# Projections q, k, v in banks of 512 columns, merged small operations, and squares summed by TensorE, in a two-layer encoder on one core

## The chip, the core and the metric

The kernel runs on one core of a Trainium2 chip. It has five engines with instruction streams of their own: TensorE (PE in the profile; its weight loads are listed as PEld), VectorE (DVE), ScalarE (ACT), GpSimd (POOL) and SyncE (SP, which issues the transfers). They meet through semaphores. On-chip tiles have 128 partitions; TensorE adds into 8 banks of PSUM, each of 128 x 512 fp32. The metric is device microseconds (us) of one execution, lower is better.

## What is computed

An encoder of two layers over 512 tokens of width 1024. A layer, cut to what matters here:

```
h = rms_norm(x, norm1_g[l]) * (1.0 + sc1) + sh1
proj = h @ w_in[l]
da_q, da_k, da_v, dn_q, dn_k, dn_v, dn_z, dn_b, dn_a, gates = split(proj)
q = apply_rope(rms_norm(q, qn_gain)); k = apply_rope(rms_norm(k, kn_gain))   # 4 heads x 2 maps x 64
p = softmax(q k^T * d**-0.5); a = p[map 0] - lam * p[map 1]; y_a = rms_norm(a @ v) ...
y_b = gated_deltanet(dn_q, dn_k, dn_v, dn_z, dn_b, dn_a)   # conv of 5 taps, chunks of 64, 4 heads, 2 directions
x = x + gt1 * ((g_a * (y_a @ w_branch_a) + g_b * (y_b @ w_branch_b)) @ w_out)
h = rms_norm(x, norm2_g[l]) * (1.0 + sc2) + sh2
x = x + gt2 * (square(relu(h @ w_mlp1)) @ w_mlp2)
```

## The kernel before

Every fp32 operand of a large product is split in a high part, rounded to the format that TensorE multiplies fast, and the low rest (hh and hl for the activations, whi and wlo for the weights, uho and ulo in the second matrix of the MLP). A product is three matmuls: hh with whi, hl with whi, hh with wlo. ScalarE makes a high part, VectorE the rest. Weights arrive in chunks of 512 KB (raw_*), 128 x 1024 elements each.

The program doesn't run in the order in which it is written. Every operation is recorded in a plan, and a list scheduler (`Plan.schedule`) puts the operations of each engine in one fixed order, from estimated costs and from levels of urgency; `Plan.issue` writes them out, so every instruction in the profile stands on line 431 and is told by its tiles. An engine works its list off strictly in that order. Pools of tiles (F for weights, Y for activations, Z for small vectors, B for the 8 banks) and limits on groups (three banks for dense products, group "d"; four chunks each of raw, whi and wlo) are part of the plan. The string ORDER (line 490), one per layer, sets the order in which the pieces of the middle of a layer are recorded: q, k, v are the projections for attention (`da_qk`, `da_v`); d is the projection of one delta-rule head and its convolution (`dn_proj`: the bank is d_dn, the running sum on VectorE is cacc, its SiLU times it is kqv); a, b, c are the steps of the delta rule (`gdn_a`, `gdn_b`, `gdn_c`); z its gate, t attention of one head. The digit is the head, or in q, k, v before the half of the columns.

- `da_dense(kind, j)` (line 801) makes one of q, k, v for 256 of its 512 columns: two chunks of 4 k-blocks x 256 columns, two banks (tokens 0 to 255 and 256 to 511, two 256-column token tiles in each), 96 matmuls. There are 12 such calls, 1152 matmuls.
- `da_qk` takes each bank: ScalarE squares it (dsq), VectorE sums the squares (dass), multiplies by cosine (rot) and by sine (dt, twice), GpSimd adds. Then `rsqrt` makes the scale (dars) from dass: a chain of 12 small VectorE operations (tiles rqv, rqu, rqr) by bit tricks and Newton steps. For k GpSimd multiplies rot by it, for q it goes into qsc. TensorE transposes rot (qkT).
- `gdn_a` needs a head's kqv: products of k with itself (kk) and q (kq), transposes (tokT, qT), another `rsqrt`, small scales (gsv, gsL and others, one operation for each of the two directions d), and L.
- `attention` has, for each of 16 tiles of queries a layer, a reciprocal of two sums (rc), a copy (r), and two multiplications (cc) before the two softmax maps are joined (pr).
- `norm` needs the sum of squares of the new x over the 1024 features. `square` (line 616) lets ScalarE square each of the 8 blocks per token half (nsq) and VectorE add it to a running sum; one matmul against ones per 128 tokens (nss) finishes it, `rsqrt` follows, nrb spreads the result over partitions, and xn, hh, hl are made. At the boundary of the layers the last blocks come out of `finish` (line 1443) one by one: transposes yT, xT, square.

Of the kernel before, what the change touches and what calls it, by code (L numbers as in the profile page):

```python
# [17 lines left out]
P = 128  # L18
# [149 lines left out]

class Eng:
# [15 lines left out]
class Plan:  # L185
# [68 lines left out]
    def schedule(self):  # L254
# [9 lines left out]
        dve_rows, dve_end = None, -OTHER_ROWS  # L264
        order = []
# [53 lines left out]
        while todo:  # L319
# [117 lines left out]
OTHER_ROWS = 110.0  # L437
DMA_LEAD, DMA_TAIL, DMA_STEP, DMA_DEPTH = 1100.0, 2400.0, 475.0, 8
# [12 lines left out]
def cost(eng, fn, dst, ins, kw):  # L451
# [21 lines left out]
    if fn == "memset":  # L473
# [4 lines left out]
NF, NY, NZ = 20, 58, 64  # L478
# [11 lines left out]
ORDER = ("q0 d0 a0 d1 a1 d2 a2 d3 a3 b0 k0 z0 c0 z1 c1 k1 z2 q1 v0 t0 z3 t1 c3 c2 v1 t2 t3",  # L490
         "d0 q0 k0 d1 a1 d2 a0 a2 d3 a3 b0 z0 c0 z1 c1 k1 z2 c2 v0 t0 q1 z3 v1 c3 t2 t3 t1")
# [3 lines left out]
def encoder(ctx, tc, a, out):  # L495
# [120 lines left out]
    def square(first, xk, hf):  # L616
# [156 lines left out]
    for l in range(DEPTH):  # L773
# [27 lines left out]
        def da_dense(kind, j):  # L801

            ch = [chunk(a["w_da"][l, 2 * kind + j, i], f"da{kind}{j}{i}") for i in range(2)]
            pss = [B([P, 2, 256], "d_da", grp="d") for tp in range(2)]
            for i in range(2):
                wh, wl = ch[i]
                for t in range(NT):
                    for k in range(4 * i, 4 * i + 4):
                        for n, (xx, w) in enumerate(((hh, wh), (hl, wh), (hh, wl))):
                            acc(pss[t // 2], t % 2, xx[k][:, t * P:(t + 1) * P], w[k % 4],  # L810
                                t % 2 == 1 and k == NK - 1 and n == 2, level=DENSE)
            return pss

        def da_qk(kind, j):
            for tp, ps in enumerate(da_dense(kind, j)):
                pl.level = EVAC
                tt = slice(2 * tp, 2 * tp + 2)
                X = ps.rearrange("p t (g d) -> p t g d", d=64)
                sq = Y([P, 8, 64], "dsq", keep=KEEP1)
                act.activation(sq.rearrange("p g d -> p (g d)"), ps.rearrange("p t c -> p (t c)"), AF.Square)  # L820
                ss = Z([P, 8], "dass")
                dve.reduce_sum(ss, sq, axis=AX.X)
                t1 = Y([P, 2, 4, 64], "rot", keep=KEEP1)
                t2 = Y([P, 2, 4, 64], "dt2", keep=KEEP1)
# [13 lines left out]
                pt = B([P, 2, 2, P], "qkT")
                for h2 in range(2):
                    for t in range(2):  # L840
                        pe.transpose(pt[:, h2, t], t1[:, t, 2 * h2:2 * h2 + 2].rearrange("p m d -> p (m d)"), ident)
                xt = Y([P, 2, 256], "qkst", keep=KEEP1)
                act.copy(xt, pt.rearrange("p h t f -> p h (t f)"))
                sp.dma_start(out=qkd[kind][:, 2 * j:2 * j + 2, 256 * tp:256 * tp + 256], in_=xt)
                pl.level = CHAIN

        def da_v(j):
            for tp, ps in enumerate(da_dense(2, j)):
                vs_ = Y([P, 2, 256], "vst", keep=KEEP1)
                act.copy(vs_, ps, level=EVAC)  # L850
                gate["v"] = sp.dma_start(out=vtd[:, 2 * tp:2 * tp + 2, 256 * j:256 * j + 256], in_=vs_, level=EVAC)
# [120 lines left out]
        def gdn_a(h, XA):  # L972
# [17 lines left out]
            for d in range(2):  # L990
                dve.tensor_tensor(out=sv[:, d], in0=rk, in1=beta[:, d, :, h], op=ALU.mult)
# [562 lines left out]
```

## Time and profile before

| | us |
|---|---|
| median of 3 runs | 1637.55 |
| lowest, highest run | 1634.5, 1638.19 |
| the profiled execution's own time | 1637.45 |
| span of its trace, first to last instruction | 1635.7 |
| TensorE busy in the span | 1597.4 (98%) |
| VectorE busy | 1314.3 (80%) |
| ScalarE busy | 829.7 (51%) |
| GpSimd busy | 164.9 (10%) |

The profile gives, for one execution, the busy time of each engine, the chain of work that ended last followed back from the end, the waits of an engine with what released it, and single instructions on a timeline with their start and duration in us. The windows view gives busy times between two moments and the granted clock of TensorE as a share of full speed (PEclk). A matmul's own duration overlaps its neighbours', so the rate of a stream is read from an unbroken stretch of it on the chain: its time over its count.

### The profile page before, as it was taken

To read this page: it belongs to the slowest core of one execution; us is meant where nothing else is said; L and a number is where in the kernel's file an instruction comes from. 1 tells how busy PE (TensorE), PEld (TensorE's weight loads), DVE (VectorE), ACT (ScalarE), POOL (GpSimd) and SP (SyncE) were. 2 spreads that over 40 slices of the span, in tenths; PEclk is the share of its full clock that TensorE was granted. 3 is DMA by queue.
4 is the path that set the end of the run, shared out by engine and by line. 5 is a ranking of instruction groups with operands and counts; after the bars stand their busy time and mean duration, and the time that the engine had idled before them with its cause. 6 is when DMAs were issued, how large, how long until landed. Compare 5 with 4: busy or idle time off the path is not lost.

```text
span 1635.7 us, 25251 instructions
## 1 busy us (share of the span) xinstructions
PE 1597.4 (98%) x9136; PEld 1385.3 (85%) x9136; DVE 1314.3 (80%) x2878; ACT 829.7 (51%) x1591; POOL 164.9 (10%) x170
## 2 busy tenths in 40 slices
PE   6989999999999999999989899999999999999998
PEld 5869988888899888888879799998888988888887
DVE  7999969899899988585998897699527885767676
ACT  4583335573266545454558442467423674636361
POOL 0253201000300000000005221000003000000000
PEclk9989999999999999999989999999999999999999
DMA  9423465538767483436233323422343525252542
GB/s 376 165 75 120 136 221 145 170 116 296 284 251 290 173 303 121 162 122 235 96 129 123 111 90 109 131 69 81 103 142 129 206 91 189 94 191 92 192 168 77
DMA packets 107726, 260.77 MB, mean 159 GB/s; under 512 B 27841, under 2 KB 40769, under 8 KB 107602
## 3 DMA queue, kind: packets, MB, share of 16 engines
q1 hardware_dynamic: 107602, 259.16, 46.1%
q8 instruction: 72, 1.18, 0.3%
q14 instruction: 52, 0.43, 0.1%
HBM read 242.31 MB, written 16.81 MB: 158 GB/s over the span
## 4 chain that ended last, share of the span: by engine, by line
PE 93%; DVE 4%; ACT 1%; issue 0%; DMA 0%; POOL 0%; SPq 0%; DVEq 0%; ACTq 0%
PE d_m L431 19%; PE d_g L431 11%; PE m2x L431 11%; PE d_da L431 8%; PE d_dn L431 6%; PE d_out L431 6%; PE m2y L431 5%; PE d_m1f L431 3%; PE d_z L431 3%; PE m2z L431 3%; PE d_brb L431 3%; PE d_bra L431 3%; PE sc L431 2%; PE px L431 2%; PE po L431 2%; PE pv L431 2%
## 5 line engine op out<-in xcount | busy, mean ns | idle before, releaser
L431 PE MATMUL d_m<-hh,whi_m 128*128 128x512 f32 x448 | 174.5, 389 | 0.0
L431 PE MATMUL d_m<-hl,whi_m 128*128 128x512 f32 x448 | 174.4, 389 | 0.0
L431 PE MATMUL d_m<-hh,wlo_m 128*128 128x512 f32 x448 | 174.4, 389 | 0.0
L431 DVE TENSOR_TENSOR m2lo<-m,m2hi 128x1024 fp32r<-128x1024 f32 x112 | 132.9, 1221 | 13.1 <-ACT m2hi L431 8.6
L431 ACT CAST m2hi<-m 128x1024 fp32r<-128x1024 f32 x112 | 114.8, 1048 | 50.1 <-DMA m<-in_w_m_dram 20.2
L431 DVE SCALAR_TENSOR_TENSOR ada<-ada,cb 128x1024 f32<-128x1024 f32 x96 | 116.5, 1227 | 2.6 <-DMA ada<-in_ada_w_dram 2.6
L431 PE MATMUL d_da<-whi_da,hh 128*128 128x256 f32 x384 | 109.4, 285 | 0.0
L431 PE MATMUL d_da<-whi_da,hl 128*128 128x256 f32 x384 | 109.1, 284 | 0.0
L431 PE MATMUL d_da<-wlo_da,hh 128*128 128x256 f32 x384 | 108.8, 285 | 0.0
L431 ACT ACTIVATE relu<-d_m 128x512 f32<-128x512 f32 x56 | 33.5, 598 | 147.8 <-PE d_m L431 147.8
L431 PE MATMUL d_g<-hh,wlo_g 128*128 128x512 f32 x256 | 102.0, 399 | 0.0
L431 PE MATMUL d_g<-hl,whi_g 128*128 128x512 f32 x256 | 102.0, 399 | 0.0
L431 PE MATMUL d_g<-hh,whi_g 128*128 128x512 f32 x256 | 102.0, 398 | 0.0
L431 PEld LDWEIGHTS d_m<-hh,wlo_m 128*128 128x128 f32 x448 | 84.1, 188 | 17.4
L431 PEld LDWEIGHTS d_m<-hh,whi_m 128*128 128x128 f32 x448 | 84.1, 188 | 17.4
L431 PEld LDWEIGHTS d_m<-hl,whi_m 128*128 128x128 f32 x448 | 84.1, 188 | 17.4
L431 PE MATMUL d_dn<-hh,whi_dn 128*128 128x512 f32 (+1 forms) x208 | 78.4, 387 | 2.6 <-DVE L L431 2.6
L431 PE MATMUL d_dn<-hh,wlo_dn 128*128 128x512 f32 (+1 forms) x208 | 79.3, 385 | 1.6 <-DVE wlo_dn L431 1.6
L431 DVE TENSOR_TENSOR u<-relu 128x256 f32<-128x256 f32 x64 | 27.1, 423 | 66.8 <-ACT relu L431 66.5
L431 PE MATMUL d_dn<-hl,whi_dn 128*128 128x512 f32 (+1 forms) x208 | 80.5, 387 | 0.0
L431 ACT CAST whi_m<-raw_m 128x1024 fp32r<-128x1024 f32 x56 | 58.7, 1049 | 42.3 <-DMA raw_m<-in_w_mlp_dram 35.7
L431 DVE TENSOR_TENSOR wlo_m<-raw_m,whi_m 128x1024 fp32r<-128x1024 f32 x56 | 67.9, 1221 | 12.6 <-ACT whi_m L431 12.4
(326 smaller groups left out, 4777.9 us busy)
## 6 DMA issues: line engine op xcount, KB each, us to landing
m<-in_w_m_dram SPq DMA_DIRECT2D x112, 512.0 KB, 4.3
ada<-in_ada_w_dram SPq DMA_DIRECT2D x96, 512.0 KB, 6.1
raw_m<-in_w_mlp_dram SPq DMA_DIRECT2D x56, 512.0 KB, 4.6
raw_g<-in_w_g_dram SPq DMA_DIRECT2D x32, 512.0 KB, 4.4
raw_out<-in_w_out_dram SPq DMA_DIRECT2D x32, 512.0 KB, 4.3
raw_dn<-in_w_dn_dram SPq DMA_DIRECT2D x24, 512.0 KB, 6.3
raw_da<-in_w_da_dram SPq DMA_DIRECT2D x24, 512.0 KB, 3.9
xs<-xT SPq DMA_DIRECT2D x24, 256.0 KB, 2.5
```

Of the source, the lines that this page charges most:

```text
L431: op.ins = getattr(eng[op.eng[0]], fn)(*[real(v) for v in op.args], **{k: real(v) for k, v in op.kw.items()})
```

## The change

1. `da_dense(kind)` makes all 512 columns of q, k or v at once: four chunks of 2 k-blocks x 512 columns, which stay through two passes, one for each pair of token tiles; a pass fills two banks of one token tile x 512 columns. A matmul has 512 columns, 96 for one kind in one layer, 576 in all. Six calls stand where twelve stood.
2. `da_qk` joins `rsqrt` for the two banks of a pass: 8 chains on 128x16 in place of 16 on 128x8 (12 operations each), 4 qsc in place of 8.
3. `gdn_a` makes gsv and gsL for both directions in one operation each: 16 in place of 32.
4. `attention` takes the reciprocal of the second sum alone and joins the two cc multiplications; the first sum's reciprocal is taken once for a head: 64 operations fewer, 8 added. In all VectorE has 2604 instructions in place of 2784, TensorE 7786 in place of 8354.
5. At the end of layer one the second token half's last four squares are not added by VectorE; TensorE sums them: 20 nss instructions in place of 12 at the boundary and 4 nsq additions fewer.
6. The planner's ORDER, two pool sizes (F 20 to 21, Y 58 to 56) and the estimate for narrow fp32 products are new; so all that stands in the middle of a layer has another order.

```diff
-ORDER = ("q0 d0 a0 d1 a1 d2 a2 d3 a3 b0 k0 z0 c0 z1 c1 k1 z2 q1 v0 t0 z3 t1 c3 c2 v1 t2 t3",
-         "d0 q0 k0 d1 a1 d2 a0 a2 d3 a3 b0 z0 c0 z1 c1 k1 z2 c2 v0 t0 q1 z3 v1 c3 t2 t3 t1")
+ORDER = ("q0 d0 d2 a2 a0 d1 a1 d3 a3 b0 k0 z1 z0 c0 z2 c2 c1 v0 z3 c3 t0 t3 t2 t1",
+         "q0 d0 d1 a0 d2 a1 a2 d3 k0 a3 b0 z0 c0 z1 z2 c1 v0 t3 c2 z3 c3 t2 t0 t1")
@@ square @@
-    def square(first, xk, hf):
+    def square(first, xk, hf, apart=False):
 
         sq = Y([P, S // 2], "nsq")
         act.activation(sq, xk[:, HALF[hf]], AF.Square)
         if first:
             nsum[hf] = [sq]
+        elif apart:
+            nsum[hf].append(sq)
         else:
             dve.tensor_tensor(out=nsum[hf][0], in0=nsum[hf][0], in1=sq, op=ALU.add)
...
@@ da_dense, da_qk @@
-        def da_dense(kind, j):
-
-            ch = [chunk(a["w_da"][l, 2 * kind + j, i], f"da{kind}{j}{i}") for i in range(2)]
-            pss = [B([P, 2, 256], "d_da", grp="d") for tp in range(2)]
-            for i in range(2):
-                wh, wl = ch[i]
-                for t in range(NT):
-                    for k in range(4 * i, 4 * i + 4):
...
+        def da_dense(kind):
+
+            ch = [chunk(a["w_da"][l, kind, i], f"da{kind}{i}") for i in range(4)]
+            for tp in range(2):
+                pss = [B([P, 512], "d_da", grp="d") for b in range(2)]
+                for i, (wh, wl) in enumerate(ch):
+                    for b, ps in enumerate(pss):
+                        ts = slice((2 * tp + b) * P, (2 * tp + b + 1) * P)
+                        for k in range(2 * i, 2 * i + 2):
+                            for n, (xx, w) in enumerate(((hh, wh), (hl, wh), (hh, wl))):
+                                pe.matmul(ps, lhsT=xx[k][:, ts], rhs=w[k % 2], start=k == 0 and n == 0,
+                                          stop=k == NK - 1 and n == 2, level=DENSE)
+                yield tp, pss
...
-                ss = Z([P, 8], "dass")
-                dve.reduce_sum(ss, sq, axis=AX.X)
...
+                ss, rs = Z([P, 2, 8], "dass"), Z([P, 2, 8], "dars")
...
                 rsqrt(rs, ss, 1.0 / 64)
...
@@ gdn_a @@
-            for d in range(2):
-                dve.tensor_tensor(out=sv[:, d], in0=rk, in1=beta[:, d, :, h], op=ALU.mult)
-                dve.scalar_tensor_tensor(out=sL[:, d], in0=sv[:, d], scalar=-1.0, in1=rk, op0=ALU.mult, op1=ALU.mult)
+            dve.tensor_tensor(out=sv, in0=beta[:, :, :, h], in1=bc(rk, 1, 2), op=ALU.mult)
+            dve.scalar_tensor_tensor(out=sL, in0=sv, scalar=-1.0, in1=bc(rk, 1, 2), op0=ALU.mult, op1=ALU.mult)
@@ attention @@
-                rc, cc = Z([P, 2], "rc"), Z([P, 1], "cc")
-                dve.reciprocal(rc, sums)
-                dve.tensor_copy(r0[:, qt:qt + 1], rc[:, 0:1])
-                dve.tensor_tensor(out=cc, in0=sums[:, 0:1], in1=rc[:, 1:2], op=ALU.mult)
-                dve.tensor_tensor(out=cc, in0=cc, in1=nlam, op=ALU.mult)
+                rc, cc = Z([P, 1], "rc"), Z([P, 1], "cc")
+                dve.reciprocal(rc, sums[:, qt, 1:2])
+                dve.scalar_tensor_tensor(out=cc, in0=sums[:, qt, 0:1], scalar=nlam, in1=rc, op0=ALU.mult, op1=ALU.mult)
...
+            dve.reciprocal(r0, sums[:, :, 0])
@@ finish @@
-                            square(m == 4 * th, xT[m], th)
+                            square(m == 4 * th, xT[m], th, th and i == 0)
```

Three places show how the planned order moves. A row is a line of the program, the operation, its output and inputs by tile and number, its size, and "xN" where N equal rows follow each other.

**VectorE in layer one, convolutions of the delta-rule heads.** In the kernel before, these rows follow the scales of the second head; kqv1_1144 and kqv0_1162 are that head's.

```order
L431 SCALAR_TENSOR_TENSOR ada0_16_450,mod0_160<-ada0_16_450,cb_103 128x1024
L431 SCALAR_TENSOR_TENSOR kqv1_1144<-kqv1_1144,cacc_770 128x512
L431 SCALAR_TENSOR_TENSOR kqv0_1162<-kqv0_1162,cacc_867 128x512
L431 COPY tok1_1179<-tokT_1169 128x512
L431 SCALAR_TENSOR_TENSOR cacc_1166<-d_dn2_876,cols_88,cacc_1166 128x510
L431 SCALAR_TENSOR_TENSOR cacc_1173<-d_dn1_975,cols_88,cacc_1173 128x510
```

The same place in the changed kernel:

```order
L444 TENSOR_SCALAR qsc_880<-dars_1106 128x2x4x2
L444 SCALAR_TENSOR_TENSOR ada0_16_450,mod0_160<-ada0_16_450,cb_103 128x1024
L444 SCALAR_TENSOR_TENSOR kqv2_1144<-kqv2_1144,cacc_910 128x512
L444 SCALAR_TENSOR_TENSOR cacc_1149<-d_dn1_1060,cols_88,cacc_1149 128x510
L444 SCALAR_TENSOR_TENSOR cacc_1155<-d_dn1_328,cols_88,cacc_1155 128x510
L444 COPY tok2_1172<-tokT_1162 128x512
L444 SCALAR_TENSOR_TENSOR cacc_1149<-d_dn1_1060,cols_88,cacc_1149 128x511
L444 SCALAR_TENSOR_TENSOR cacc_1155<-d_dn1_328,cols_88,cacc_1155 128x511
L444 SCALAR_TENSOR_TENSOR cacc_1149<-d_dn1_1060,cols_88,cacc_1149 128x511
```

The scales of the whole of q stand ahead now, and the sum over the late bank d_dn1_1060 stands in front of the sum over d_dn1_328, a bank that TensorE fills much earlier.

**TensorE in layer two, around the second head's kk.** Before, with two projections (d_dn2_9769, d_dn1_9794) begun and the third weight parts not yet used, and the transposes qkT of k's first half behind it:

```order
L431 MATMUL d_dn2_9769<-hl0_8828,whi_dn20_9737 128x512
L431 MATMUL d_dn1_9794<-hh0_8821,whi_dn10_9747 128x512
L431 MATMUL d_dn1_9794<-hl0_8828,whi_dn10_9747 128x512
L431 MATMUL kk_9808<-kqv1_9799 128x128 x4
L431 MATMUL tokT_9819<-cst_86,kqv1_9799 128x128 x4
L431 MATMUL d_dn0_9835<-hh0_8821,whi_dn00_9757 128x512
L431 MATMUL d_dn0_9835<-hl0_8828,whi_dn00_9757 128x512
L431 MATMUL d_dn2_9769<-hh0_8821,wlo_dn20_9829 128x512
L431 MATMUL d_dn2_9769<-hh1_8841,whi_dn20_9737 128x512
L431 MATMUL d_dn2_9769<-hl1_8857,whi_dn20_9737 128x512
L431 MATMUL qkT_9854<-cst_86,rot_9587 128x128 x2
```

In the changed kernel:

```order
L444 MATMUL d_dn2_9199<-hl6_8507,whi_dn20_9135 128x512
L444 MATMUL d_dn2_9199<-hh6_8500,wlo_dn20_9181 128x512
L444 MATMUL d_dn2_9199<-hh7_8505,whi_dn20_9135 128x512
L444 MATMUL d_dn2_9199<-hl7_8512,whi_dn20_9135 128x512
L444 MATMUL kk_9279<-kqv1_9264 128x128 x4
L444 MATMUL tokT_9291<-cst_86,kqv1_9264 128x128 x4
L444 MATMUL d_dn2_9199<-hh7_8505,wlo_dn20_9181 128x512
L444 MATMUL d_dn1_9299<-hh0_8429,whi_dn10_9144 128x512
L444 MATMUL d_dn1_9299<-hl0_8444,whi_dn10_9144 128x512
L444 MATMUL d_dn1_9299<-hh0_8429,wlo_dn10_9284 128x512
```

The kk stands at the end of a full projection, with no qkT behind it: all of q has been made ahead of it, and k comes later.

**TensorE at the boundary of the layers.** Before:

```order
L431 MATMUL yT<-cst,y_6490 128x128 x4
L431 MATMUL m2y<-m2lo,uho 128x512
L431 MATMUL yT<-cst,y_6517 128x128
L431 MATMUL nrb<-cst,nrs 128x128 x2
L431 MATMUL yT<-cst,y_6517 128x128 x3
L431 MATMUL nss<-ones,nsq 128x1 x2
L431 MATMUL d_ba<-hh_8821,w_ba 32x256
L431 MATMUL d_dn_8836<-hh_8821,whi_dn_8638 128x256
L431 MATMUL d_ba<-hl_8828,w_ba 32x256
L431 MATMUL d_dn_8836<-hl_8828,whi_dn_8638 128x256
```

In the changed kernel:

```order
L444 MATMUL yT<-cst,y_6071 128x128 x4
L444 MATMUL yT<-cst,y_6098 128x128 x4
L444 MATMUL nss<-ones,nsq 128x1 x2
L444 MATMUL nrb<-cst,nrs 128x128 x2
L444 MATMUL nss<-ones,nsq 128x1 x8
L444 MATMUL d_ba<-hh_8429,w_ba 32x256
L444 MATMUL d_da<-whi_da_8230,hh_8429 128x512 x2
L444 MATMUL d_ba<-hl_8444,w_ba 32x256
```

Eight nss stand between the last transposes and the next layer's first products, and 512-column products of q on the first token half stand where 256-column products of the delta rule's projection stood.

## Rows read from the trace of the kernel before

**Rows 1.** The page: span, busy time and share of engines, the chain by engine.

```profile
span 1635.7 us, 25251 instructions
PE 1597.4 (98%) x9136; PEld 1385.3 (85%) x9136; DVE 1314.3 (80%) x2878; ACT 829.7 (51%) x1591; POOL 164.9 (10%) x170
PE 93%; DVE 4%; ACT 1%; issue 0%; DMA 0%; POOL 0%; SPq 0%; DVEq 0%; ACTq 0%
```

**Rows 2.** Windows: stretch, busy us of PE, PEld, DVE, ACT, POOL; clock; DMA; GB/s.

```profile
50.00:135.60 85.60, 79.36 (x433) 67.04 (x432) 78.85 (x226) 57.50 (x159) 27.12 (x27) 0.92 0.29 91
135.60:372.00 236.40, 236.40 (x1682) 212.67 (x1681) 208.34 (x621) 116.57 (x274) 34.53 (x40) 1.00 0.48 150
...
820.00:850.00 30.00, 24.70 (x160) 22.19 (x160) 26.17 (x79) 18.59 (x43) 3.58 (x6) 0.83 0.42 147
850.00:912.00 62.00, 55.09 (x374) 50.72 (x373) 51.03 (x159) 42.00 (x114) 28.16 (x23) 0.96 0.27 88
912.00:1160.00 248.00, 248.00 (x1711) 223.00 (x1710) 213.51 (x639) 126.22 (x308) 31.85 (x44) 1.00 0.34 104
```

**Rows 3.** Pieces of the chain, in order: start us, us, what.

```profile
179.03 18.60 PE d_da L431 x155
...
577.70 43.52 PE d_m L431 x192
...
980.78 13.44 PE d_da L431 x112
```

**Rows 4.** Waits of TensorE, 95 to 135 us: us in total, times, longest us.

```profile
PE d_dn L431 <- DVE L L431: 2.6, 1, 2.6
PE qT L431 <- DVE kqv L431: 1.9, 1, 1.9
PE tokT L431 <- DVE kqv L431: 1.7, 1, 1.7
```

**Rows 5.** Costliest groups, VectorE and ScalarE: count | busy us, mean ns of one | idle before.

```profile
L431 DVE TENSOR_TENSOR wlo_da<-raw_da,whi_da 128x1024 fp32r<-128x1024 f32 x24 | 29.2, 1218 | 1.6 <-ACT whi_da L431 1.6
L431 DVE TENSOR_TENSOR dt<-d_da,sgn 128x256 f32<-128x256 f32 x32 | 12.7, 414 | 0.0
L431 DVE TENSOR_REDUCE dass<-dsq 128x8 f32<-128x512 f32 x16 | 11.4, 716 | 1.4 <-ACT dsq L431 1.4
L431 DVE TENSOR_TENSOR rot<-d_da,cg 128x512 f32<-128x512 f32 x16 | 10.9, 684 | 1.4 <-ACT dsq L431 1.4
L431 DVE TENSOR_TENSOR cc<-sums,rc 128x1 f32<-128x1 f32 x32 | 5.6, 175 | 0.0
L431 ACT ACTIVATE dsq<-d_da 128x512 f32<-128x512 f32 x16 | 9.5, 599 | 21.6 <-PE d_da L431 20.2 <-issue 1.4
```

**Rows 6.** Waits of TensorE, 850 to 912 us.

```profile
PE kk L431 <- DVE rqr L431: 3.6, 1, 3.6
PE qkT L431 <- POOL rot L431: 1.7, 1, 1.7
PE d_dn L431 <- DVE wlo_dn L431: 1.6, 1, 1.6
```

**Rows 7.** Timeline there: start us, duration us, instruction, [wait before it].

```profile
897.73 0.24 DVE L431 SCALAR_TENSOR_TENSOR rqu<-rqr 128x8 f32<-128x8 f32 x2
904.39 4.77 POOL L431 TENSOR_TENSOR rot<-rot,dars 128x512 f32<-128x512 f32 x2 [9.02 <-DVE dars L431]
```

**Rows 8.** Waits of TensorE, 820 to 850 us.

```profile
PE nss L431 <- DVE nsq L431: 3.4, 1, 3.4
PE yT L431 <- DVE y L431: 1.9, 1, 1.9
```

**Rows 9.** Timeline there.

```profile
831.87 0.42 ACT L431 ACTIVATE nsq<-xT 128x256 f32<-128x256 f32 x1 [0.31 <-DVE xT L431]
833.08 0.42 DVE L431 TENSOR_TENSOR nsq<-nsq 128x256 f32<-128x256 f32 x1
833.64 0.99 PE L431 MATMUL nss<-ones,nsq 128*128 128x1 f32 x4 [3.42 <-DVE nsq L431]
```

More of the change, by code (lines that the diff above doesn't have):

```diff
@@ L370, in schedule @@
                     s = max(s, dve_end + OTHER_ROWS)
+            elif e == "pe":
+                rows = op.form()
+                if rows != pe_form:
+                    s = max(s, pe_end + OTHER_FORM)
             if e == "pe":
@@ L396, in schedule @@
                     dve_rows, dve_end = rows, op.end
+                elif e == "pe":
+                    pe_form, pe_end = rows, op.end
             order.append(op)
@@ L437 @@
 OTHER_ROWS = 110.0
+OTHER_FORM = 0.0
 DMA_LEAD, DMA_TAIL, DMA_STEP, DMA_DEPTH = 1100.0, 2400.0, 475.0, 8
@@ new lines, in da_qk @@
+        def da_qk(kind):
+            for tp, pss in da_dense(kind):
+                pl.level = EVAC
+                ss, rs = Z([P, 2, 8], "dass"), Z([P, 2, 8], "dars")
+                t1s = []
+                for b, ps in enumerate(pss):
+                    t = 2 * tp + b
+                    X = ps.rearrange("p (g d) -> p g d", d=64)
+                    sq = Y([P, 8, 64], "dsq", keep=KEEP1)
+                    act.activation(sq.rearrange("p g d -> p (g d)"), ps, AF.Square)
+                    dve.reduce_sum(ss[:, b], sq, axis=AX.X)
+                    t1 = Y([P, 8, 64], "rot", keep=KEEP1)
+                    t2 = Y([P, 8, 64], "dt2", keep=KEEP1)
+                    dve.tensor_tensor(out=t1, in0=X, in1=bc(cg[:, kind, t], 1, 8), op=ALU.mult)
+                    dve.tensor_tensor(out=t2[:, :, 0:32], in0=X[:, :, 32:64], in1=bc(sg[:, kind, t, 0:32], 1, 8), op=ALU.mult)
+                    dve.tensor_tensor(out=t2[:, :, 32:64], in0=X[:, :, 0:32], in1=bc(sg[:, kind, t, 32:64], 1, 8), op=ALU.mult)
+                    pool.tensor_tensor(out=t1, in0=t1, in1=t2, op=ALU.add)
+                    t1s.append(t1)
@@ L838, in da_qk @@
[L838 to L844, printed above, removed]
-                pl.level = CHAIN
[L847 to L851, printed above, removed]
+                for b, t1 in enumerate(t1s):
+                    if kind:
+                        pool.tensor_tensor(out=t1, in0=t1, in1=bc(rs[:, b], 2, 64), op=ALU.mult)
+                    pt = B([P, H, P], "qkT")
+                    for h in range(H):
+                        pe.transpose(pt[:, h], t1[:, 2 * h:2 * h + 2].rearrange("p m d -> p (m d)"), ident)
+                    xt = Y([P, H, P], "qkst", keep=KEEP1)
+                    act.copy(xt, pt)
+                    t = 2 * tp + b
+                    sp.dma_start(out=qkd[kind][:, :, t * P:(t + 1) * P], in_=xt)
@@ L854, in encoder, with da_v @@
+                pl.level = CHAIN
+        def da_v():
+            for tp, pss in da_dense(2):
+                for b, ps in enumerate(pss):
+                    vs_ = Y([P, 512], "vst", keep=KEEP1)
+                    act.copy(vs_, ps, level=EVAC)
+                    gate["v"] = sp.dma_start(out=vtd[:, 2 * tp + b], in_=vs_, level=EVAC)
         kqv, ztile = {}, {}
@@ L1261, in encoder @@
             elif kind in "qk":
-                da_qk("qk".index(kind), h)
+                da_qk("qk".index(kind))
             elif kind == "v":
-                da_v(h)
+                da_v()
             else:
```

41 lines of the change are left out of this document (12 added, 29 removed).

## The prediction, made before the changed kernel ran

> **What bounds the kernel now.** I read the page first: TensorE is busy 98% of the span, and the chain of waits is 93% TensorE and 4% VectorE [rows 1]. So time can come from two places alone: from TensorE's work itself, or from the stretches where it stands. The windows say where it stands [rows 2]. Between 135 and 372 us, and between 912 and 1160 us, it is busy for the whole stretch at the full clock (1.00, that is 2.4 GHz), with VectorE at 208 of 236 and 214 of 248 us beside it. Three stretches differ. 50 to 135.6 us: idle 85.60 - 79.36 = 6.24 us, mean granted clock 0.92; 820 to 850 us: idle 5.30 us, clock 0.83; 850 to 912 us: idle 6.91 us, clock 0.96. A mean below 1 here is a time at the lower level (1.2 GHz) behind the idle time. Taken as (1 - clock) x stretch, it costs up to 6.8, 5.1 and 2.5 us. Together these stretches lose up to 13.1, 10.4 and 9.4 us. The views of waits name what ended last there: VectorE in all but one [rows 4, 6, 8].
>
> The profiled execution took 1637.45 us, 1.75 us more than its span and 0.1 us under the median of the runs; the sum below is made against it and needs no correction. A measurement of this kernel can tell about 0.2%, 3.3 us, from no change.
>
> **The change, part by part.**
>
> *512 columns.* The rate of a stream is read off unbroken pieces of the chain: 155 matmuls of 256 columns in 18.60 us and 112 in 13.44 us, both 0.1200 us each; 192 of 512 columns in 43.52 us, 0.2267 us each [rows 3]. So each takes its columns at the full clock and 13.3 ns more. Two of 256 cost 0.2400 us, one of 512 costs 0.2267 us: 0.0133 us less, for 576 of them 7.7 us. All of this is on the path, since TensorE is the bound where they stand, but for those in the stretches that wait. I take -7.7 us. Apart from that: by the Trainium skill ("TensorE: Matmul & The Clock Gate", section "Back-to-back issue gap") one isolated matmul costs its columns at 2.4 GHz and about 2.5 ns more, so a pair would save 2.5 ns, by an estimate from that page 1.4 us in all. The rows speak against it: 0.1200 us for 256 columns is 13 ns above the columns, not 2.5.
>
> *Layer one, 50 to 135 us.* TensorE waits 2.6 + 1.9 + 1.7 us here [rows 4], for L and kqv: VectorE is behind. Up to the last head's kk the changed order gives TensorE all of q in place of half: 96 x 0.2267 - 96 x 0.1200 = +10.2 us. VectorE gets two more wlo_da (2 x 1.22) and the reading of two more banks' worth (dass 0.72, rot 0.68, two dt of 0.41, so 2.23 each) [rows 5], and some half us less of merged scales: +6.4 us. TensorE's cover grows by 3.8 us. That would leave 2.4 of the 6.2 us of waiting, and the slow clock behind it. But the order on VectorE takes some of it back: the sum over d_dn1_1060 now stands ahead of four sums and a kqv whose bank has long been full, so VectorE idles until TensorE comes to that bank. Everything queued behind it on VectorE, the later kqv and then L, is put off with it. I take -4, all of the cover and none of the clock. The ends are 0, when VectorE's forced idle time eats the cover, and -10.6, when the clock stays up as well.
>
> *Layer two, 850 to 912 us.* Waits of 3.6 us for a VectorE chain at the second head's kk, 1.6 us for wlo_dn and 1.7 us for GpSimd's rot, in this order [rows 6]. Two scale chains run interleaved in front (two operations take 0.24 us [rows 7]), and GpSimd multiplies k's rot by the scale for 4.77 us after 9.02 us of waiting for it [rows 7], with qkT behind. In the changed order q is whole before this kk and k comes later. So there are two 12-step chains in place of four ahead (24 x 0.12 = 2.9 us less on VectorE), the GpSimd step is gone from here, and TensorE has 3.0 us more work up to this kk (19 more products of 512 columns in d_dn, 4.3 us, less the 1.3 us by which 96 products of q at 0.2267 are cheaper than 192 of two halves at 0.1200). Cover grows by 2.9 + 3.0 = 5.9 of the 6.9 us. A wlo_dn still stands right behind the kk, so not all of it goes. I take -6; the ends are -2 (only the GpSimd wait goes) and -9.4 (all of it).
>
> *Boundary, 820 to 850 us.* nss waits 3.4 us for nsq, behind a wait of 1.9 us for y [rows 8]. The last square ends at 832.29 us and its addition only at 833.50, with nss at 833.64 [rows 9]. Without the four additions (0.42 each, in one queue with xT and xn) nss can follow the square: 1.2 us sooner, and xn sooner too. Against it stand eight nss of some 0.25 us in place of four, of which only the last two wait for the last square. The next matmuls are 512-column products of q on one token half, which need one hh for longer. I take -2.5; the ends are +1 (the eight products in a row, 8 x 0.25 less the 1 us of before) and -6.5 (nss's wait and more than half of the clock's 5.1 us).
>
> *Middle of the layers.* 180 VectorE operations are gone; at 0.12 to 0.18 us each [rows 5, 7] that is 22 to 32 us less work on it. TensorE doesn't wait there [rows 2], so I cost this at nothing: TensorE's own dense products hide it, and if they ran out it would be a gain. New there is the handover. Both banks of a pass end within six matmuls of each other, 1.4 us, where before they ended 24 matmuls apart, 2.9 us; and the four weight chunks come free only in the second pass, so the next kind's splits (a wlo is 1.22 us) crowd into its end. I put +1 us on it, between -2 and +6. The nearest row is the 0 us of idle time at d_da [rows 2].
>
> Sum: 1637.45 - 7.7 - 4 - 6 - 2.5 + 1 = 1618.25, so **1618 us**.
>
> **The rivals.**
>
> *B, the merge alone pays: 1637.45 - 7.7 = 1630 us.* The stalls are not lack of cover but order: VectorE's fixed list makes it idle at d_dn1_1060 and then lag by as much as before, and at the boundary rsqrt and y bind as before. For it: the order in layer one, and that VectorE is the releaser of nearly all waits [rows 4, 6, 8], so a small error in its order comes back in full. Against it: the cover is counted in whole projections, and GpSimd's rot is surely gone from the second kk. With a few us of handover on top it ends within 0.2% of no change.
>
> *C, slower: 1648 us.* The handover of banks becomes the bound. There are three banks for dense products; a pass takes two that end nearly together, so the second bank of the next pass can only start when the first of this one has been read. Between the two stand some 21 matmuls, 4.8 us. The reading takes dsq 0.60, dass 0.72, rot 0.68 and two dt of 0.41, 2.8 us [rows 5], plus whatever stands ahead on VectorE. It decides from 4.8 + 20.2/12 = 6.5 us: 12 passes would then eat the 20.2 us gained, which takes three wlo (3.7 us) in front of the reads each time. At 2.6 us a pass, with the clock falling behind it, it is 1618 + 12 x 2.5 = 1648. For it: VectorE is 88% busy there. Against it: d_da ran 155 products without a gap under the same limit [rows 3], and VectorE has less to do.
>
> *D, the fixed 13.3 ns is no property of a matmul* but of the two-tile banks or the weight loads in d_da and d_m, and halving the number of matmuls saves next to nothing: 1618 + 6.3 = 1624 us. This is what the page cited above would make of it. For it: no row here shows a 512-column stream with q's operands. Against it: the same 13.3 ns is left over at both sizes [rows 3].
>
> **How the numbers follow.** The forecast has 0.66, B 0.24 (0.17 of it faster, 0.07 within 0.2%), C 0.06, D 0.04. Faster: 0.66 + 0.17 + 0.04 = 0.87; the same 0.07; slower 0.06. The forecast's own terms run from 1637.45 - 7.7 - 10.6 - 9.4 - 6.5 - 2 = 1601 to 1637.45 - 7.7 + 0 - 2 + 1 + 6 = 1635, but the ends don't fall together; half of each way gives about 1609 to 1627. The range reaches up over B's 1630 to 1632 and leaves out C, B's dearer part and a tail below 1608, about 2 in 10.
>
> **What would show it.** Unbroken pieces of d_da at 0.2267 us: the first term. In layer one the waits for kqv and L down from 6.2 to about 2 us, with VectorE idle ahead of cacc from d_dn1_1060; if that idle time is 9 us or more and TensorE's waits are unchanged, B is right there. In layer two no qkT waiting for rot before the second head's kk, and the clock at 1.00 for 850 to 912 us. At the boundary nss waiting for the ScalarE square, not for VectorE. In the middle, d_da waiting for rot, dt or dass would be C, and d_da waiting for wlo_da the dear end of the handover. The prediction is wrong if the three stretches keep their idle time, or if TensorE, now at 1.00, gets gaps between 135 and 372 us.

## The result, and the profile after

The changed kernel takes 1624.80 us (median of 4 runs, 1623.97 to 1625.94) against 1636.03 us (1634.5 to 1638.19) of the kernel before (the three runs of the table above and a fourth of 1634.5 us): a ratio of 0.9931, interval 0.9914 to 0.9948. That is 11.2 us less. The profiled execution took 1624.73 us, 12.7 us less than that of before. The forecast was 1618 us in a range of 1608 to 1632: the sign and the range hold, and the time is 6.8 us above the likeliest value.

The page of the changed kernel answers to [rows 1]: span, busy time of each engine, the chain by engine.

```profile
span 1622.6 us, 23945 instructions
PE 1587.8 (98%) x8576; PEld 1349.6 (83%) x8576; DVE 1292.1 (80%) x2698; ACT 830.8 (51%) x1595; POOL 161.8 (10%) x170
PE 89%; DVE 5%; ACT 3%; DMA 2%; issue 1%; SPq 0%; POOL 0%; DVEq 0%; ACTq 0%; POOLq 0%
```

The windows answer to [rows 2], in the same columns (stretch, busy us of PE, PEld, DVE, ACT, POOL; clock; DMA; GB/s):

```profile
50.00:135.60 85.60, 79.92 (x395) 63.78 (x393) 76.35 (x208) 58.12 (x153) 26.82 (x24) 0.98 0.27 88
135.60:372.00 236.40, 236.14 (x1456) 202.71 (x1456) 211.08 (x566) 118.88 (x288) 32.83 (x44) 1.00 0.47 148
...
820.00:850.00 30.00, 27.99 (x152) 21.65 (x151) 23.71 (x81) 18.90 (x45) 5.16 (x7) 0.94 0.13 46
850.00:912.00 62.00, 56.62 (x322) 49.73 (x320) 43.21 (x115) 45.13 (x116) 21.10 (x15) 0.94 0.41 128
912.00:1160.00 248.00, 246.77 (x1527) 212.75 (x1526) 205.62 (x586) 128.33 (x316) 37.87 (x51) 1.00 0.35 105
```

At the boundary the idle time fell from 5.30 to 2.01 us. In layer one it is 5.68 us where it was 6.24, in layer two 5.38 where it was 6.91. These two stretches were to give 10 of the 19 us. TensorE's waits name other operations than [rows 4], [rows 6] and [rows 8] did: for 95 to 135 us, for 850 to 912 us, and for 820 to 850 us (us in total, times, longest us):

```profile
PE d_dn L444 <- DVE wlo_dn L444: 2.6, 1, 2.6
PE tokT L444 <- DVE kqv L444: 2.1, 1, 2.1
PE qT L444 <- DVE kqv L444: 0.8, 1, 0.8
...
PE kk L444 <- DVE kqv L444: 5.4, 1, 5.4
...
PE yT L444 <- DVE y L444: 0.8, 1, 0.8
PE nrb L444 <- DVE nrs L444: 0.6, 1, 0.6
PE d_ba L444 <- ACT hh L444: 0.5, 1, 0.5
```

The pieces of the chain (start us, us, what) answer to [rows 3]: 0.2273 and 0.2271 us for each product of 512 columns in two pieces of k and v, beside 0.2267 in d_m. q's own pieces on the chain are shorter, 29 products at most.

```profile
154.48 18.18 PE d_da L444 x80
174.23 17.03 PE d_da L444 x75
...
653.45 43.52 PE d_m L444 x192
```

**A finer measure.** The ends of matmuls are modelled, so that a busy share of 100% hides short gaps. For what follows I took all starts of TensorE's matmuls from each trace, and for each the distance to the next start, less the distance at which its shape follows itself where nothing holds it up (0.2267 us for 512 columns, 0.1200 for 256, and so on). The sum over a stretch is called its loss here; it holds the slow clock too. Only differences of it are used. The borders are the same in all kernels. In us:

| kernel | 50–200 | 200–372 | 372–785 | 785–850 | 850–912 | 912–1160 | whole span |
|---|---|---|---|---|---|---|---|
| before | 12.9 | 10.1 | 1.7 | 10.2 | 10.2 | 9.4 | 73.5 |
| after | 11.1 | 10.3 | 1.2 | 6.9 | 8.7 | 10.6 | 67.6 |
| e1, no gb exponentials | 10.5 | 10.8 | 1.2 | 9.2 | 3.2 | 10.7 | 64.6 |
| e2, decay blocks late in layer two | 11.0 | 10.6 | 1.2 | 7.7 | 1.5 | 8.8 | 59.9 |
| e3, late in both layers | 5.2 | 22.1 | 0.6 | 8.2 | 1.8 | 9.8 | 66.8 |
| e4, old order | 14.4 | 15.3 | 0.6 | 7.6 | 13.1 | 8.9 | 80.1 |
| e5, new order alone | 17.9 | 10.6 | 1.7 | 9.4 | 6.0 | 10.3 | 75.7 |
| e6, not merged | 11.8 | 13.0 | 1.2 | 8.4 | 8.5 | 13.1 | 74.3 |
| e7, squares on VectorE | 11.2 | 10.7 | 1.2 | 9.4 | 9.7 | 10.8 | 71.0 |
| e8, a middle level in layer one too | 7.2 | 11.6 | 1.4 | 7.9 | 0.8 | 9.6 | 56.5 |
| e9, e1 with a copy moved | 10.5 | 10.8 | 1.2 | 7.6 | 3.8 | 10.4 | 63.7 |
| e10, before, with blocks late in layer two | 12.7 | 10.3 | 1.8 | 10.3 | 0.7 | 11.3 | 67.0 |

From before to after the loss falls by 5.9 us and the span by 13.1. The other 7.2 us are TensorE's own work as counted, matmuls times their undisturbed distances: some 7.7 us less for the wide products, and a little more for the added nss. So this number is worked out from the rates and is no second measurement of them.

How far one trace can be trusted shows where TensorE's order is the same. Up to 785 us the changed kernel, e1, e2, e7 and e9 agree within 0.7 us in each stretch. At the boundary, 785 to 850 us, the changed kernel, e1, e2 and e9 have one order and still lose 6.9 to 9.2 us; the last section says why. The trace of e8 is of its fastest run, 2.8 us under its median.

**Layer two, where most of the gain stayed out.** The kk that waits is now that of the first head, and VectorE, which releases it, has itself waited 16.56 us for ScalarE. ScalarE's timeline, and the rows of VectorE and TensorE that follow (start us, duration us, instruction, [wait before it]):

```profile
868.54 0.62 ACT L444 ACTIVATE w<-w 128x512 f32<-128x512 f32 x1
869.06 0.62 ACT L444 ACTIVATE gb<-gb 128x512 f32<-128x512 f32 x1
869.58 1.27 ACT L444 ACTIVATE w<-gb,ngcum 128x128 f32<-128x128 f32 x4
...
882.86 0.97 ACT L444 ACTIVATE w<-gb,ngcum 128x128 f32<-128x128 f32 x3
883.73 0.61 ACT L444 ACTIVATE kqv<-cacc 128x512 f32<-128x512 f32 x1
...
866.57 0.75 DVE L444 SCALAR_TENSOR_TENSOR cacc<-d_dn,cols,cacc 128x510 f32<-128x510 f32 x1
884.38 0.69 DVE L444 SCALAR_TENSOR_TENSOR kqv<-kqv,cacc 128x512 f32<-128x512 f32 x1 [16.56 <-ACT kqv L444]
...
885.12 2.07 PE L444 MATMUL kk<-kqv 128*128 128x128 f32 x8 [5.38 <-DVE kqv L444]
```

The SiLU's input cacc is complete at 867.3 us. ScalarE starts the SiLU at 883.73, behind seven decay blocks and part of an eighth: |gb + ngcum| in four pieces, exp of w, exp of gb, some 2.2 us a block. They run in the same place before (874.63 to 893 us), but there the first head's kk has long run:

```profile
855.93 1.05 PE L431 MATMUL kk<-kqv 128*128 128x128 f32 x8
```

In the changed order all of q stands in front, and this kk comes as late as the blocks.

### The profile page after: what moved, and what is told of

It reads as the page before. It is cut to its first block, busy times and chain, and to the rows that moved or that the text cites. A ratio compares the mean times of both kernels' runs of the same rounds, so it can differ in the third digit from the quotient of the medians.

```text
span 1622.6 us, 23945 instructions
## 1 busy us (share of the span) xinstructions
PE 1587.8 (98%) x8576; PEld 1349.6 (83%) x8576; DVE 1292.1 (80%) x2698; ACT 830.8 (51%) x1595; POOL 161.8 (10%) x170
## 4 chain that ended last, share of the span: by engine, by line
PE 89%; DVE 5%; ACT 3%; DMA 2%; issue 1%; SPq 0%; POOL 0%; DVEq 0%; ACTq 0%; POOLq 0%
PE d_m L444 19%; PE m2x L444 11%; PE d_g L444 11%; PE d_da L444 7%; PE d_out L444 6%; PE m2y L444 5%; PE d_dn L444 4%; PE d_m1f L444 3%; PE d_z L444 3%; PE d_brb L444 3%; PE m2z L444 3%; PE d_bra L444 3%; PE px L444 2%; PE sc L444 2%; PE po L444 2%; PE pv L444 2%
## 5 line engine op out<-in xcount | busy, mean ns | idle before, releaser
L444 DVE TENSOR_TENSOR m<-m,m 128x1024 f32<-128x1024 f32 x64 | 77.4, 1217 | 0.0
L444 PE MATMUL d_da<-whi_da,hl 128*128 128x512 f32 x192 | 76.0, 396 | 0.0
L444 DVE TENSOR_TENSOR wlo_m<-raw_m,whi_m 128x1024 fp32r<-128x1024 f32 x56 | 67.7, 1220 | 10.2 <-ACT whi_m L444 10.1
L444 PE MATMUL d_da<-whi_da,hh 128*128 128x512 f32 x192 | 75.7, 397 | 0.0
```

What stands on the lines that cost most here:

```text
L444: op.ins = getattr(eng[op.eng[0]], fn)(*[real(v) for v in op.args], **{k: real(v) for k, v in op.kw.items()})
```

## The experiments

**e1: theory S (ScalarE's queue sets the kk of layer two) against the order of VectorE.** The exp of gb is not issued, so that q lacks its decay factor; all orders are kept:

```diff
-                act.activation(gb, gb, AF.Exp)
+                gex = act.activation(gb, gb, AF.Exp)
+                gex.parts = []
```

> Leaves out the exponentials of gb on ScalarE (16 operations of 0.62 us, 0.52 us apart, eight in each layer), so q's decay factor is wrong; no other engine's order changes. Theory S (ScalarE's queue): in layer two the first head's kk waits 5.4 us because its SiLU (kqv on ScalarE) stands behind seven decay blocks, each with one gb exponential. Then the SiLU comes 7 x 0.52 = 3.6 us sooner and the wait for kqv falls from 5.4 to about 1.8 us. In layer one VectorE's wait of 3.2 us for kqv goes, and TensorE's waits of 0.8 + 2.1 + 2.6 us between 118 and 136 us fall by about 3 us. Time about 1618 us against the changed kernel's 1624.8. Rival V (VectorE's own work, as the prediction had it): both stretches keep their waits, 1624 to 1625 us.

Measured: 1620.78 us, ratio 0.9905 (0.9891 to 0.9920), 4.0 us less than the changed kernel. The waits of VectorE and of TensorE in layer two, and VectorE's in layer one:

```profile
DVE kqv L449 <- ACT kqv L449: 12.2, 1, 12.2
...
PE kk L449 <- DVE kqv L449: 1.1, 1, 1.1
...
DVE tok L449 <- PE tokT L449: 1.6, 1, 1.6
```

Seven operations of 0.6 us fewer ahead of the SiLU make VectorE's wait 4.4 us shorter and the kk's wait 4.3 us. The loss of layer two goes from 8.7 to 3.2: S holds there. In layer one VectorE's wait for the SiLU falls from 3.2 to 0.2 us too, but another takes its place, for TensorE at the copy of tok, and the loss falls by 0.6 us only, where I had expected 3.

**e2, e3, e8: the blocks run later, nothing left out.** A level is the planner's urgency; CHAIN is the most urgent of these, and the blocks had it, ahead of the SiLU. With 1.5 they stand ahead of the weight splits, with 2.5 behind them.

```diff
+                wl = 2.5 if l else CHAIN
-                    act.activation(w[:, t], gb[:, t], AF.Abs, bias=ngcum[:, d, t, h:h + 1])
-                act.activation(w, w, AF.Exp, scale=-1.0)
+                    act.activation(w[:, t], gb[:, t], AF.Abs, bias=ngcum[:, d, t, h:h + 1], level=wl)
+                act.activation(w, w, AF.Exp, scale=-1.0, level=wl)
...
-                act.activation(gb, gb, AF.Exp)
+                act.activation(gb, gb, AF.Exp, level=wl)
```

e2 is this; e3 has `wl = 2.5` in both layers; e8 has `wl = 2.5 if l else 1.5`.

> The decay blocks of layer two (w and gb on ScalarE) get a lower urgency in the plan, so that the SiLU of the heads and the weight splits stand ahead of them; up to the first block the order is the changed kernel's. The transfer of gb lands no sooner. Theory S: the wait of kk for kqv in layer two falls from 5.4 to under 1 us, VectorE's 16.6 us of idle time ahead of it goes, 850 to 912 us loses some 2 to 3 in place of 8.7 us: about 1619 us. Rival D (the late transfer of gb is what counts, 866 us): the wait stays at several us. Rival V: 1624 to 1625 us. Layer one is the same in all.

> The same in both layers. Theory S for layer one too: there VectorE loses 3.2 us on the SiLU behind eight decay blocks and TensorE waits 5.6 us in all; without it some 3 us less: about 1616 us, if the new order of the whole of layer one brings nothing else. Rival V: layer one is bound by VectorE's sums themselves, the waits stay and the time is that of the layer-two change alone, about 1619.

> As e2 in layer two; in layer one the decay blocks stand behind the SiLU of the heads but ahead of the weight splits. Theory: in e3 the waits at 100 to 150 us went (9.1 to 0.5 us lost) and came back as 11.7 us in the triangular inverse at 190 to 240 us, since the blocks and with them L came late. With the blocks ahead of the splits, L is earlier than in e3 and most of layer one's 9 us is gained: 1610 to 1613 us. Rival: any later L is given back at the inverse, or VectorE's sums bind by themselves: 1617 us or more, as e2.

Measured: e2 1617.44 us, 0.9888 (0.9871 to 0.9904); e3 1622.08, 0.9914 (0.9899 to 0.9929); e8 1616.17, 0.9886 (0.9871 to 0.9901). The first two rows are layer two and its kk in e2. The third is layer one in e3, and the last two are what follows it there:

```profile
850.00:912.00 62.00, 61.58 (x356) 53.47 (x355) 56.84 (x138) 47.08 (x119) 22.40 (x20) 1.00 0.50 158
871.03 1.16 PE L444 MATMUL kk<-kqv 128*128 128x128 f32 x8 [0.42 <-DVE kqv L444]
...
100.00:136.00 36.00, 36.00 (x187) 30.33 (x186) 35.80 (x87) 25.08 (x65) 15.84 (x16) 1.00 0.25 76
...
200.00:220.00 20.00, 17.26 (x130) 13.98 (x128) 11.79 (x20) 4.10 (x9) 1.06 (x2) 1.00 0.74 240
220.00:240.00 20.00, 16.62 (x125) 14.52 (x124) 13.47 (x34) 5.41 (x15) 0.99 (x2) 0.83 0.37 114
```

e2 gains 7.4 us, nearly all of it in layer two (8.7 to 1.5): the kk comes 14 us sooner and waits 0.4 us. So the gain that I had forecast for layer two was there to be had, and ScalarE's queue kept it out. e1 shows this with every order kept; e2's level also moves TensorE's order, from 869 us on. In e3 layer one loses 5.9 us less than in the changed kernel, but the blocks are then late for the triangular inverse, and 200 to 372 us lose 11.8 us more. A level between the two (e8) gets 3.9 us of the first and pays 1.3 us of the second. Against e2 that is 1.3 us less in the median, which the intervals can't tell from nothing. I had expected 1616 us of e3 and 1610 to 1613 of e8; both came out higher. e2 and e8 are faster than both kernels of this case.

**e4 and e5: the parts apart.** e4 is the changed kernel with the order of before: the whole q, k, v stand where the first halves stood, and the pool Z has 60 places, not 64. e5 is the kernel before with the new order, both halves where the whole stands.

```diff
-ORDER = ("q0 d0 d2 a2 a0 d1 a1 d3 a3 b0 k0 z1 z0 c0 z2 c2 c1 v0 z3 c3 t0 t3 t2 t1",
-         "q0 d0 d1 a0 d2 a1 a2 d3 k0 a3 b0 z0 c0 z1 z2 c1 v0 t3 c2 z3 c3 t2 t0 t1")
+ORDER = ("q0 d0 a0 d1 a1 d2 a2 d3 a3 b0 k0 z0 c0 z1 c1 z2 v0 t0 z3 t1 c3 c2 t2 t3",
+         "d0 q0 k0 d1 a1 d2 a0 a2 d3 a3 b0 z0 c0 z1 c1 z2 c2 v0 t0 z3 c3 t2 t3 t1")
```

> The changed kernel with the pieces in the order of before (whole q, k, v where the first halves stood; pool Z 60 for lack of room). If the new order of pieces carries the gain of the stretches, layer one loses about 12.9 us again and layer two about 10 (second head's kk), the 512-column products keep their 7.7 us: 1628 us. If the whole q in front carries it, layer one loses about 11 as in the changed kernel. In layer two the first head's kk stands ahead of the decay blocks here, so theory S expects no wait of 5 us for kqv at the first head.

```diff
-ORDER = ("q0 d0 a0 d1 a1 d2 a2 d3 a3 b0 k0 z0 c0 z1 c1 k1 z2 q1 v0 t0 z3 t1 c3 c2 v1 t2 t3",
-         "d0 q0 k0 d1 a1 d2 a0 a2 d3 a3 b0 z0 c0 z1 c1 k1 z2 c2 v0 t0 q1 z3 v1 c3 t2 t3 t1")
+ORDER = ("q0 q1 d0 d2 a2 a0 d1 a1 d3 a3 b0 k0 k1 z1 z0 c0 z2 c2 c1 v0 v1 z3 c3 t0 t3 t2 t1",
+         "q0 q1 d0 d1 a0 d2 a1 a2 d3 k0 k1 a3 b0 z0 c0 z1 z2 c1 v0 v1 t3 c2 z3 c3 t2 t0 t1")
```

> The kernel before, with 256-column products, unmerged small operations and VectorE's additions at the boundary, in the changed kernel's order of pieces (both halves of q, k, v where the whole stands). Theory A: 576 pairs cost 0.0133 us more each, so 7.7 us of TensorE's work more than the changed kernel; the waits in layer two (kk for kqv behind the decay blocks) are there as well: about 1632 us or somewhat more, with the boundary's additions. Rival D (the 13.3 ns are not saved by halving the number of products): about 1625 us. That the new order alone would carry the change: 1625 us too, told from D by the rate of d_da, 0.1200 us in either case.

Measured: e4 1637.01 us, 1.0005 (0.9996 to 1.0015): no change. e5 1639.27 us, 1.0025 (1.0016 to 1.0034): slower by about 4 us. Neither half pays alone; I had expected 1628 us of e4 and 1632 or somewhat more of e5. e4 doesn't tell the order from the smaller pool. In it no kk of layer two waits for kqv, as S expects, but TensorE waits there for GpSimd's rot (first row), six times as long as in [rows 6]. In e5 the wait for nsq at the boundary stays (second row), and layer one loses 17.9 us:

```profile
PE qkT L444 <- POOL rot L444: 10.4, 2, 7.8
...
PE nss L431 <- DVE nsq L431: 3.7, 1, 3.7
PE qT L431 <- DVE kqv L431: 2.8, 1, 2.8
```

**e6: the merged operations taken apart again.** The changed kernel with its order kept; each merged operation of VectorE (scales of q and k, gsv and gsL, reciprocals and cc) is issued as the two or three it was made of. The edit is one list for each such operation; the one for the scales:

```diff
-                rsqrt(rs, ss, 1.0 / 64)
+                rsqrt(rs, ss, 1.0 / 64, True)
```

> The changed kernel with the 176 merged VectorE operations put back, each pair in the place of the merged one, and no other engine's order changed (the first sum's reciprocal is still taken once for a head). Theory: under the dense products they cost nothing; in layer one, where VectorE has no idle time from 103 to 136 us, some 30 of them stand ahead of the last head's kk, 0.08 to 0.15 us each: TensorE waits 2 to 4 us more there: 1627 to 1629 us. Rival N: they cost nothing anywhere, 1624.8. Rival F: they count in full, 176 x 0.08 = 14 us: 1639.

Measured: 1631.06 us, 0.9973 (0.9963 to 0.9983): 6.3 us slower than the changed kernel, for 176 operations. Busy time and chain:

```profile
PE 1594.4 (98%) x8576; PEld 1350.9 (83%) x8576; DVE 1303.8 (80%) x2874; ACT 831.0 (51%) x1595; POOL 163.0 (10%) x170
PE 81%; DVE 13%; ACT 2%; DMA 2%; issue 1%; POOL 1%; SPq 0%; DVEq 0%; ACTq 0%; POOLq 0%
```

VectorE has 11.7 us more work, and 6.3 us of it reach the end. Its share of the chain goes from 5% to 13%. Layer one, where I had expected the cost, loses 0.7 us more; 200 to 372 us lose 2.7 and 912 to 1160 us 2.5 more. The list of TensorE's waits is empty in the first of these and has 1.0 us in the second, no more than the 1.2 us of the changed kernel. So it is many gaps too short for a list of waits. I had costed these operations at nothing.

**e7: the last four squares added by VectorE again.**

```diff
-                            square(m == 4 * th, xT[m], th, th and i == 0)
+                            square(m == 4 * th, xT[m], th)
```

> The changed kernel with the last four squares added by VectorE again (12 nss at the boundary). Theory: nss waits for the additions again, 1.2 to 3.4 us at 820 us, and xn starts later: 1626 to 1628 us. Rival O: the boundary's 3.3 us came from the other order of products there (512-column products while hh arrives), not from the squares: 1625 us.

Measured: 1627.94 us, 0.9954 (0.9940 to 0.9967), 3.1 us slower, and the boundary's old wait is back with 2.5 us (below), which rival O did not expect. From the boundary on the planner orders anew, and layer two loses 1.0 us more. The loss of the boundary itself, 9.4 us, lies too near to the 6.9 to 9.2 us of the four traces above to measure the squares.

```profile
PE nss L444 <- DVE nsq L444: 2.5, 1, 2.5
PE nrb L444 <- DVE nrs L444: 1.1, 1, 1.1
```

**e9: is layer one bound by the amount of VectorE's work?** e1, with one copy of tok moved to ScalarE:

```diff
-                        ad.copy(tok, pt)
+                        tc_ = ad.copy(tok, pt)
+                        if (l, h, part) == (0, 0, 2):
+                            tc_.parts = "act"
```

> The kernel without q's decay exponentials (16 ScalarE operations left out, so q's decay is wrong), with one more edit: one tok copy of layer one runs on ScalarE and not on VectorE, all orders else unchanged. Theory V: layer one is bound there by VectorE, which runs from 103 to 136 us with no gap but the 1.60 us for the copy. Then VectorE gains 1.60 + 0.69 = 2.3 us, and the program ends near 1618.5. Rival T: what TensorE loses between 100 and 136 us is set by TensorE's own order (forced idle from dependences in its own queue), so that the wait moves to the next operation: 1620.8, as without the edit.

Measured: 1620.56 us, 0.9902 (0.9888 to 0.9917), as e1. This agrees with T in the time, but VectorE's waits in layer one show that the edit took with one hand what it gave with the other: the wait for tokT is gone, and ScalarE, now with the copy, is waited for.

```profile
DVE cacc L452 <- ACT cacc L452: 1.5, 1, 1.5
DVE kqv L452 <- ACT kqv L452: 1.0, 1, 1.0
```

So the run doesn't tell T from V. e3 does speak against V: there VectorE was busy for 35.80 of 36 us and TensorE for all 36.00. What waits for what in layer one is a matter of order among three engines; which of the three orders is the one to mend stays open.

**e10: the edit of e2 in the kernel before.** As the diff of e2, in the kernel before.

> The kernel before, with nothing changed but the urgency of layer two's decay blocks (level 2.5, the edit that gave 7.4 us in the changed kernel). Theory S: in the changed kernel the edit paid because the first head's SiLU stood behind these blocks; in the kernel before the first head's k is long done when they run (kk near 846, blocks 874 to 892 us), so the time stays near 1636 (1634 to 1638). Rival G: a lower urgency of these blocks is good in any order, because it clears ScalarE for all of layer two: then some 7 us less, near 1629.

Measured: 1629.93 us, 0.9962 (0.9948 to 0.9976): 6.1 us faster, as rival G had it, where S as I had put it expected no change. (The first head's kk, which the expectation puts near 846 us, stands at 856.) Layer two loses 0.7 us in place of 10.2; 1.9 of these come back between 912 and 1160 us. Rows of before, ScalarE and VectorE, and the window of e10:

```profile
871.75 1.04 ACT L431 CAST whi_dn<-raw_dn 128x1024 fp32r<-128x1024 f32 x1
874.63 1.56 ACT L431 ACTIVATE w<-gb,ngcum 128x128 f32<-128x128 f32 x5
...
894.25 0.70 ACT L431 ACTIVATE cacc<-d_dn,cols 128x512 f32<-128x512 f32 x1
894.82 2.97 ACT L431 CAST whi_dn<-raw_dn 128x1024 fp32r<-128x1024 f32 x3
...
894.98 0.75 DVE L431 SCALAR_TENSOR_TENSOR cacc<-d_dn,cols,cacc 128x510 f32<-128x510 f32 x1 [2.38 <-ACT cacc L431]
...
850.00:912.00 62.00, 62.00 (x416) 56.95 (x415) 56.47 (x168) 45.48 (x119) 26.59 (x23) 1.00 0.34 101
```

In the kernel before the blocks held up other things: ScalarE cast no weights between 872.8 and 894.8 us, and its cacc for the second head came at 894.25. VectorE waited 2.38 us for that, with the scale chain behind it that [rows 6] names at kk. In e10 casts stand between the blocks (at 881.15, 886.71 and 892.05 us). By these rows the wait for "DVE rqr" that I had read as VectorE's chain had ScalarE behind it already then. The level also moves TensorE's order, so this run alone doesn't show that ScalarE's queue is all of it; e1, with every order kept, shows it for the changed kernel. Later blocks paid in layer two in both orders, but not in layer one (e3).

## Why the forecast was right in sign and 6.8 us too low

The number is in the range, but not for all of its reasons. The two stretches that were to give 10 us gave 3.3 and kept 5.68 of 6.24 and 5.38 of 6.91 us of idle time; stretches that keep their idle time are what the prediction itself names as a sign of being wrong.

| step | forecast | measured | how |
|---|---|---|---|
| 512 columns | -7.7 | -7.2 | counted: span less loss |
| layer one | -4 | -1.8 | loss, 50–200 |
| layer two | -6 | -1.5 | loss, 850–912 |
| boundary | -2.5 | -3.3 | loss, 785–850 (-1.0 to -3.3 in four traces) |
| middle | +1 | +0.9 | loss, 200–372, 372–785, 912–1160 |
| sum | -19.2 | -12.9 | profiled: -12.7 |

*512 columns: right in the rate.* The unbroken pieces of k and v show 0.2271 to 0.2273 us where the forecast needed 0.2267. Against two halves at 0.1200 that saves 0.0127 to 0.0129 us a pair, 7.3 to 7.4 us for 576. So in these streams the 13.3 ns come once with each matmul, and rival D falls. With it falls, for these streams, the 2.5 ns that the page of the Trainium skill gives for one isolated matmul ("TensorE: Matmul & The Clock Gate", "Back-to-back issue gap"): by an estimate from it the saving would be 1.4 us. That D's 1624 us lies nearest to the measured time is luck: its term failed, and the time that it left out was lost in layers one and two. No run has the wide products alone, so that all of their saving reaches the end is argued from TensorE's share of the chain and not shown.

*Layer two: the step that failed.* I counted cover, 5.9 us of more work for TensorE and less for VectorE ahead of the second head's kk, and that kk indeed no longer waits. But I had read only VectorE and GpSimd there. The step "q is whole before this kk" also puts the first head's kk later, from 856 us to the 871 us that it has in e2, and so into the stretch in which ScalarE's queue holds 18 us of decay blocks; these put it off to 885 us. ScalarE was at 42 of 62 us in [rows 2], and I passed over it. The row to read was the instruction ahead of the SiLU in ScalarE's own timeline. Mending that alone (e2) brings the kernel to 1617.4 us.

*Layer one: too much by 2.2 us.* The mechanism named, VectorE's forced idle time at d_dn1_1060, did not occur: VectorE came there late and ran on. What the row shows is a wait for a SiLU that stood behind decay blocks, as in layer two:

```profile
103.26 0.81 DVE L444 SCALAR_TENSOR_TENSOR kqv<-kqv,cacc 128x512 f32<-128x512 f32 x1 [3.21 <-ACT kqv L444]
```

With it gone (e1), one for tokT follows. The prediction's wait for kqv is there still (2.1 and 0.8 us), the one for L has gone, and one for wlo_dn (2.6 us) has come. So the step that failed here is the idle time at that bank; what costs the 2.2 us in its place stays open.

*Boundary: right.* nss no longer waits, and in e7 its wait of 2.5 us is back and the time is 3.1 us longer. The forecast had 2.5. The 3.3 us of the table are of the trace with the highest clock of four.

*Middle: right in the sum, wrong in its parts.* "I cost this at nothing: TensorE's own dense products hide it" fails by e6: the merged operations are worth 6.3 us, some 0.036 us each, 5.2 of them in the stretches after 200 us that [rows 2] shows as fully busy. The same gaps could not be seen in a modelled busy time. Against it stands what the wide banks cost there. e5 and e6 are planned by the same ORDER, and neither has the merged operations. With the wide banks (e6) 200 to 372 us lose 2.4 us more and 912 to 1160 us 2.8 more, about 5 us, near the upper end of the "between -2 and +6" that I had given the handover. That it is the handover is not shown, since each of the two has a plan of its own. The two nearly cancel, and that +1 came out is luck.

*The rivals.* B said that the merge alone pays and order eats the rest; at 1630 us it is 5 us too high, nearer than the forecast's 6.8 us too low, and its place (d_dn1_1060) is wrong, but its idea, "not lack of cover but order", is what layers one and two show. The order on its own costs 3 to 4 us (e5); with the parts it belongs to it is worth 12 us (e4 against the changed kernel, 1637.0 to 1624.8). C, a bank handover that sets the end, did not come about: no wait of d_da on rot, dt or dass stands in the list of TensorE's waits. (Its working writes 2.6 us a pass and multiplies by 2.5.)

## What to carry to other kernels

Where a wait names an engine, look at what that engine waited for and what stood ahead of it in its queue; here kk in layer two of the changed kernel, and, as far as its rows tell, that of the kernel before, stood behind 18 us of decay exponentials that were planned ahead of need on ScalarE, an engine that is busy for half the span. So did a SiLU in layer one, but there the next wait took over when it was gone: only a run tells whether a wait sets the time. When a change moves a critical operation to another time, lay its whole chain over every engine's queue at the new time, not only the queue that released it before. And a busy share of 100% from modelled ends is no proof of cover: 176 small operations that I had taken as hidden behind it were worth more than half of this change.

## What the runs showed of the hardware that was not expected

The granted clock fell in some executions and not in others at the same place with the same order of instructions. In layer one the end did not move by it; at the boundary it did. Layer one, 118 to 136 us, e7 and e2, in which TensorE's and VectorE's rows up to the end of layer one are those of the changed kernel (e7 first):

```profile
118.00:136.00 18.00, 11.00 (x63) 8.21 (x63) 18.00 (x59) 7.12 (x24) 5.63 (x7) 1.00 0.03 4
...
118.00:136.00 18.00, 12.80 (x60) 9.39 (x59) 18.00 (x58) 7.84 (x25) 6.04 (x5) 0.81 0.01 2
```

At 1.00 TensorE is idle for 18.00 - 11.00 = 7.00 us, at 0.81 (part of the time at 1.2 GHz) for 5.20, and layer one loses 11.2 and 11.0 us. While VectorE, busy for all 18.00 us, sets the pace, a slower TensorE only fills its own idle time. The kernel before agrees: its order in layer one is also that of e10, the clock over 50 to 135.6 us was 0.92 and 0.96, and the stretch 50 to 200 us loses 12.9 and 12.7 us. I had priced the clock on top of the idle time, up to 6.8 us for layer one; the runs show nearly none of that there.

At the boundary, where the changed kernel and e1 have the same order, it is otherwise (785 to 850 us, the changed kernel first):

```profile
785.00:850.00 65.00, 62.99 (x321) 50.81 (x320) 55.58 (x135) 34.23 (x69) 6.16 (x8) 0.97 0.32 115
...
785.00:850.00 65.00, 63.57 (x307) 51.70 (x306) 53.36 (x131) 33.09 (x67) 4.75 (x7) 0.92 0.32 115
```

e1 has 0.58 us less idle time and still loses 9.2 us in place of 6.9. Its clock is 0.66 over 820 to 835 us, where TensorE is busy for 13.57 of 15 us. So where TensorE has its own work to do, the slow time counts.
